# Values of a gated attention as a second seven-product unit, with operands resting in DRAM

## The chip, the cores and the metric

The kernel runs on one core of a Trainium2 chip (trn2). The metric is the device time of one execution in microseconds. The core's engines work from queues of their own and wait for each other by semaphores: TensorE (PE in the profile) multiplies, VectorE (DVE) and ScalarE (ACT) work elementwise and empty PSUM, GpSimd (POOL) does some elementwise work and issues transfers, SyncE (SP) issues transfers. Sixteen DMA engines move the data, for whichever queue.

## The reference

One decoder layer on 512 tokens of width 1024, in float32. What matters here is the token mixer's input projection, `h @ w_in`, and who reads its sections:

```python
q_g, k_g, v_g, r_g, a_lr, q_lat, kv_lat, gate_logits = jnp.split(h @ w_in, offsets, axis=-1)
o_gla = gla_chunked(q heads, k heads, v_g heads, log_a heads)      # gated linear attention, 4 heads
o_gla = rms_norm(o_gla, gla_norm_g)
y_gla = (o_gla * jax.nn.silu(r_g)) @ w_o_gla
q  = rms_norm(q_lat, q_a_norm_g) @ w_q_b                           # latents of the second attention
kv = rms_norm(kv_lat[..., :256], kv_a_norm_g) @ w_kv_b
```

`v_g` (the values) and `r_g` (the output gates before their silu) are both 512 x 1024 products of the normalised input, 512 x 1024, with 1024 x 1024 columns of `w_in`. After the mixer come an output projection, a layer norm, an MLP of width 4096 and a last layer norm.

## The kernel before

All large products are made from float32 operands that are split in a high and a low part (`split`, line 104, and line 180/181 for weights: ACT rounds the high part, DVE subtracts). A product is then three matmuls: high x high, high x low, low x high. Tokens stand in 4 tiles of 128 (`NT`), the width in 8 blocks of 128 (`NK`). `hT` holds the normalised input, transposed, as eight tiles with both parts.

*Weights* come as a stream planned ahead (`plan`, `pump`, lines 138 to 184): an entry is a pair of row blocks by up to 512 columns, 512 KB, loaded by SP into one of three `wraw` buffers, and split into `whi`/`wlo` or, where the entry's home is "a", into `xh`/`xl`.

*The seven-product unit.* The output gates `r` are made by `proj_r` (line 678) with a scheme of seven products in place of eight quarter products (Winograd's form of Strassen's). The input's rows (tokens) are taken as two halves of 256, its width as two halves of 512, the weight's columns as two halves of 512. `r_sums` (line 624) makes four sums and differences of the input's quarters, S1 to S4, each split in two tiles. The sums of weight quarters, T1 to T4, are made by transfers: `r_load` (line 612) loads a quarter on POOL's queue into a tile `rw`, and with `accum_op` adds another to what lies there. The order is `RPH`: T1, 11, 22, T2, 21, T3, T4; 11 and 21 are quarters of the weight itself and come through SP. T2 is made in T1's tile, T4 in T2's, T3 in 22's, each once the split of the tile before has been made. Seven products of 24 matmuls each accumulate in four PSUM banks; `put` (ACT) copies a bank out, `last` (DVE) adds a second one. `silus` (line 692) then turns the four result tiles `rg` into gates in place (ACT's tanh, line 697, DVE, line 698).

*The values* are made by `proj_v` (line 599): two plain GEMMs `gemm_tm` (line 246) of 512 columns over 8 row blocks and 4 token tiles. Each evacuation splits a PSUM bank straight into `vh` and `vl` (`split`, line 605).

*Side lanes.* Other work is written as generators that a `tick` (line 208) advances by one step, at most three of them at a time in this part (`WID`, line 1104): the levels of the gated attention (`gla_levels`, line 780, four heads one after the other), its outputs (`gla_out`, line 878, which wait for a head's levels, values and gates), and the silu. The GEMMs tick after each row block, `proj_r` eight times in all. A scheduler orders each engine's queue by priority, which is the order of the program, and by readiness in a model of the time; then each queue is fixed and runs in order. The sequence of sections is `ORDER` (line 288):

```python
ORDER = (("r", 0), ("v", 0), ("v", 1), ("g", 0), ("g", 2), ("qr", 0), ("g", 1), ("g", 3), ("qr", 1))
```

Here `g` are GEMMs of the branch gates and `qr` uses the latents. `latents2` (line 559) makes those: three tiles `qlT` and two `ckT` in `rms_T` (line 497).

*Memory.* All the tiles above except `hT`, `wraw`, `whi` and `wlo` share 24 slots of 4 KB per partition under the tag "A" (line 74): `s1` to `s4`, `rw`, `xh`/`xl`, `rg`, `vh`/`vl`, `latT`, `qk`, `kq`, `sd`, `KK`, the branch gates `gt`, `ogT`. A tile takes a slot when one is free and gives it back after its last reader.

Of the kernel before, what the change touches and what calls it, by code (L numbers as in the profile page):

```python
# [52 lines left out]
def tile_hybrid_block(ctx: ExitStack, tc: tile.TileContext, I, out, dbg=None):  # L53
# [24 lines left out]

    def S(shape, dt=F32, n="s"):
        return sm.tile(shape, dt, tag=n, name=nm(n))  # L80

    def MM(n="mm"):
        return pm.tile([P, T], F32, tag="mm", name=nm(n))
# [204 lines left out]
    ORDER = (("r", 0), ("v", 0), ("v", 1), ("g", 0), ("g", 2), ("qr", 0), ("g", 1), ("g", 3), ("qr", 1))  # L288

    RPH = ("T1", "11", "22", "T2", "21", "T3", "T4")  # L290
    RW = {}
    RAHEAD, RHOME = 2, "wawawawawawaww"

    def plan_qr(g):
        PL["qr", g] = plan("w_q_b", NOPE, 4 * ROPE, heads=(HQ, 4 * g, 4), per=4)

    for sec, i in ORDER:
        if sec == "v":
            PL["v", i] = plan("w_in", C_V + i * T, T)
        elif sec == "r":  # L300
            for n, op in enumerate(RPH):
                for hf in range(2):
                    PL["r", n, hf] = len(stream)
                    if op in ("11", "21"):
                        plan("w_in", C_R, T, 4 * (op == "21") + 2 * hf, 4 * (op == "21") + 2 * hf + 2)
                    else:
                        stream.append({"src": lambda q=(op, hf): RW[q], "nk": 2, "n": T, "res": False})
                    stream[-1].update(ahead=RAHEAD, home=RHOME[2 * n + hf])
# [287 lines left out]
    Rp = [None] * 2  # L596
    ogT = [None] * NK

    def proj_v(hp, guard=None):
        vp = []  # L600

        def e(a, j, ps):
            if a % 2 == 0:
                vp.append((A([P, 2, T], F32R, "vh"), A([P, 2, T], F32R, "vl")))
            split(ps, vp[-1][0][:, a % 2, :], vp[-1][1][:, a % 2, :])
            if a == NT - 1:
                Vp[hp] = vp
        gemm_tm([PL["v", hp]], hT, T, e, guard=guard)

    RS = {}  # L610

    def r_load(op, i, j, hf, add=False):
        w = I["w_in"].rearrange("(k p) n -> p k n", p=P)
        if not add:
            RW[op, hf] = A([P, 2, T], F32, "rw")
        k0 = 4 * i + 2 * hf
        nc.gpsimd.dma_start(RW[op, hf], w[:, k0:k0 + 2, C_R + j * T:C_R + (j + 1) * T], **({"accum_op": ALU.add} if add else {}))

    def r_add(dst, src, i, j):
        for hf in range(2):  # L620
            RW[dst, hf] = RW[src, hf]
            r_load(dst, i, j, hf, add=True)

    def r_sums():
        H, L = slice(0, 256), slice(256, T)
# [15 lines left out]
        RS["S1"] = pair("s1")  # L641
        for m in range(2):
            split(X[m], *[w[:, 2 * m:2 * m + 2] for w in RS["S1"]])
            yield
        RS["S4"] = pair("s4")
        for m in range(2):
            x = X[m]
            for kk in range(2):
                for w in range(2):
                    vtt(x[:, kk], x[:, kk], f(hT[2 * m + kk][:, w, H]), op=ALU.add)  # L650
            yield
            y = B([P, 2, 256], F32, "sy")
            for kk in range(2):
                k = 2 * m + kk
                vtt(y[:, kk], x[:, kk], f(hT[k + 4][:, 0, H]), op=ALU.subtract)
                vtt(y[:, kk], y[:, kk], f(hT[k + 4][:, 1, H]), op=ALU.subtract)
            yield
            split(y, *[w[:, 2 * m:2 * m + 2] for w in RS["S4"]])
            yield
        RS["S2"] = pair("s2")  # L660
        for m in range(2):
            c = slice(2 * m, 2 * m + 2)
            split(X[m], RS["S2"][0][:, c], RS["S2"][1][:, c], scale=-1.0)
            yield
        RS["S3"] = pair("s3")
        for m in range(2):
            c = slice(2 * m, 2 * m + 2)
            y = B([P, 2, 256], F32, "sy")
            for kk in range(2):
                k = 2 * m + kk  # L670
                t = B([P, 2, 256], F32, "st")
                vtt(t, f(hT[k][:, :, H]), f(hT[k][:, :, L]), op=ALU.subtract)
                vtt(y[:, kk], t[:, 0], t[:, 1], op=ALU.add)
            yield
            split(y, RS["S3"][0][:, c], RS["S3"][1][:, c])
            yield

    def proj_r():
        a, b = [MM() for _ in range(2)], None
        b = [MM() for _ in range(2)]  # L680
        R = {}

        def put(key, t, o, scale=1.0):
            if key not in R:
                R[key] = A([P, 2, T], F32, "rg")
            act(R[key][:, t], o, AF.Copy, scale=scale)

        def last(key, t, o, op):
            r = R[key][:, t]
            vtt(r, r, o, op=op)  # L690

        def silus():
            for key in ("12", "11", "22", "21"):
                for t in range(2):
                    r = R[key][:, t]
                    th = B([P, T], F32, "th")
                    act(th, r, AF.Tanh, scale=0.5)
                    stt(r, th, 1.0, r, op0=ALU.add, op1=ALU.mult)
                    yield
            Rp[0], Rp[1] = [R["11"], R["21"]], [R["12"], R["22"]]  # L700

        def lhs(n, k, t):
# [8 lines left out]
            while key not in RS:  # L711
                step(t_rs)
            return [w[:, k, c] for w in RS[key]]

        for n in range(7):
            o = a if n in (1, 3, 5) else b
            for hf in range(2):
                pump(PL["r", n, hf])
                for pp in range(2):
                    for t in range(2):  # L720
                        xh, xl = lhs(n, 2 * hf + pp, t)
                        hi, lo = [w[:, pp] for w in stream[PL["r", n, hf]]["w"]]
                        opens = n in (0, 1, 4, 6) and hf == 0 and pp == 0
                        mm(o[t], xh, hi, start=opens, stop=False, skip_group_check=True)
                        mm(o[t], xh, lo, start=False, stop=False, skip_group_check=True)
                        mm(o[t], xl, hi, start=False, stop=hf == 1 and pp == 1, skip_group_check=True)
                if hf == 0 and n in (0, 6):
                    tick(None)
                if n == 0 and hf == 1:
                    r_add("T2", "T1", 1, 1)  # L730
                if n == 2 and hf == 1:
                    r_add("T3", "22", 0, 1)
                if n == 3 and hf == 1:
                    r_add("T4", "T2", 1, 0)
            for t in range(2):
                if n == 0:
                    put("22", t, o[t], -1.0)
# [12 lines left out]
                    last("21", t, o[t], ALU.add)  # L750
            if n < 6:
                tick(None)
        return spawn(silus())

    SS = [None] * GH

# [121 lines left out]
    def gla_out(h):  # L878
        while SS[h] is None or Vp[h // 2] is None or Rp[h // 2] is None:
            yield  # L880
        sd, s128, kq = SS[h]

        def V(j):
            c = slice(h % 2 * HV, (h % 2 + 1) * HV)
# [34 lines left out]
        og = [B([P, 2, HV], F32, "og") for _ in range(2)]  # L919
        for i in range(NT):  # L920
            o = ps[i // 2][:, (i % 2) * HV:(i % 2 + 1) * HV]
            stt(og[i // 2][:, i % 2, :], o, rs[:, i:i + 1], Rp[h // 2][i // 2][:, i % 2, h % 2 * HV:(h % 2 + 1) * HV],
                op0=ALU.mult, op1=ALU.mult)
        yield
        for kk in range(2):
# [148 lines left out]
    for hf in range(2):  # L1074
        r_load("T1", 0, 1, hf)
    r_add("T1", "T1", 0, 0)
    RS["q"] = True
    gemm_fm(PL["q"], hT, T, ev_q, width=3)
    for hf in range(2):
        r_load("22", 1, 1, hf)  # L1080
    t_lat2 = spawn(latents2())
    gemm_fm(PL["k"], hT, T, ev_k, width=3)
    finish(t_prep, t_lat)
# [24 lines left out]
    def gates(br, mb):  # L1108
# [4 lines left out]
            act(gt[m][:, br, :], ps, AF.Tanh, scale=0.5, bias=hbg[:, br * NK + m:br * NK + m + 1])  # L1113
        gemm_fm(PL["g", br, mb], hT, T, ev_g)

    for sec, i in ORDER:
        if sec == "v":
            proj_v(i)
        elif sec == "r":
            proj_r()  # L1120
            finish(t_lat2)
        elif sec == "g":
            gates(i // 2, i % 2)
        else:
            mla_qr(i)
# [377 lines left out]
```

## Time and profile before

| | |
|---|---|
| median of 3 runs | 876.64 us (876.24 to 876.95) |
| the profiled execution | 876.98 us |
| its span, first to last instruction | 875.2 us |
| mean granted clock of TensorE | 0.998 |
| gates' unit on PE | 95.1 to 139.2 us |
| values on PE | 139.5 to 192 us |

A page of the profile tells one execution. A row of a group gives line, engine, operation, tiles out<-in, shape, count, then busy time and mean length of one in ns, then the engine's idle time before them and what ended it. A row by source line gives the lengths as min/median/max and the first and last start. A row of a stretch gives, for each engine, its busy time and the number of instructions, then the granted clock (PEclk), the share of time in which the 16 DMA engines were busy, and GB/s. A row of the timeline begins with start and length in us. PEld is the load of the stationary operand, which overlaps PE.

### The profile page before, as it was taken

How to read it: one execution, taken by the hardware profiler on the slowest of the kernel's cores; microseconds unless marked ns; L12 is line 12 of the kernel's file. 1: busy time of each engine (PE TensorE's matmuls, PEld its weight loads, DVE VectorE, ACT ScalarE, POOL GpSimd, SP SyncE). 2: the span in 40 equal slices, each digit the busy share in tenths (PEclk: the TensorE clock that was granted, in tenths of full speed). 3: DMA queues.
4: the chain of work that ended last, by engine and by line, in shares of the span. 5: the costliest groups of instructions: out<-in, count | busy, mean ns of one | idle time of the engine just before them, and what ended most of it. 6: DMA issues, size and time to landing. Idle time of an engine off the chain costs nothing. (4 is left out here: it accounts for less than half of the span.)

```text
span 875.2 us, 11522 instructions
## 1 busy us (share of the span) xinstructions
PE 857.4 (98%) x4312; PEld 730.7 (83%) x4312; DVE 595.6 (68%) x979; ACT 456.2 (52%) x788; POOL 163.9 (19%) x196
## 2 busy tenths in 40 slices
PE   5999999999999999999999999999999999999996
PEld 5988888888898888888888889988888888888885
DVE  6977998665564345557776888886567556753697
ACT  5367865454554343345555414566357546744662
POOL 2404753103011010000000012004400520242023
PEclk9999999999999999999999999999999999999999
DMA  6823572222222223121216537007931990398075
GB/s 225 244 59 124 109 154 73 72 83 70 84 73 73 67 66 121 31 67 57 95 64 248 169 102 260 1 1 193 282 103 37 260 254 28 67 314 196 0 186 104
DMA packets 65080, 105.34 MB, mean 120 GB/s; under 512 B 7905, under 2 KB 31892, under 8 KB 65024
## 3 DMA queue, kind: packets, MB, share of 16 engines
q1 hardware_dynamic: 47312, 61.94, 22.1%
q0 software_dynamic: 15792, 39.00, 19.2%
q10 hardware_dynamic: 1920, 3.66, 1.2%
q8 instruction: 34, 0.56, 0.3%
q14 instruction: 22, 0.18, 0.1%
HBM read 86.76 MB, written 3.67 MB: 103 GB/s over the span
## 5 line engine op out<-in xcount | busy, mean ns | idle before, releaser
L181 DVE TENSOR_TENSOR wlo<-wraw,whi 128x1024 fp32r<-128x1024 f32 (+2 forms) x96 | 109.3, 1139 | 128.4 <-ACT whi L180 122.4
L231 PE MATMUL mm<-h,whi 128*128 128x512 f32 x416 | 163.0, 393 | 0.0
L232 PE MATMUL mm<-h,whi 128*128 128x512 f32 x416 | 162.3, 390 | 0.0
L233 PE MATMUL mm<-h,wlo 128*128 128x512 f32 x416 | 155.0, 391 | 0.0
L180 ACT ACTIVATE whi<-wraw 128x1024 fp32r<-128x1024 f32 (+2 forms) x96 | 93.6, 975 | 100.3 <-PE mm L232 47.0
L1365 POOL DMA_DIRECT2D res<-ev x54 | 47.2, 983 | 238.5 <-ACT ev L1363 197.2
L233 PEld LDWEIGHTS mm<-h,wlo 128*128 128x128 f32 x416 | 78.0, 188 | 16.0
L231 PEld LDWEIGHTS mm<-h,whi 128*128 128x128 f32 x416 | 78.2, 188 | 15.6
L232 PEld LDWEIGHTS mm<-h,whi 128*128 128x128 f32 x416 | 78.2, 188 | 15.5
L1430 ACT ACTIVATE relu<-mm 128x512 f32<-128x512 f32 x32 | 18.8, 595 | 57.0 <-PE mm L233 57.0
L370 POOL TENSOR_TENSOR mv<-mv,mhalf 128x1 f32<-128x1 f32 x4 | 2.9, 744 | 208.1 <-DVE mv L369 208.1
L180 ACT ACTIVATE xh<-wraw 128x1024 fp32r<-128x1024 f32 (+1 forms) x22 | 21.1, 968 | 27.0 <-PE mm L266 15.8
L181 DVE TENSOR_TENSOR wlo<-wq,whi 128x1024 fp32r<-128x1024 f32 x15 | 18.4, 1224 | 20.4 <-ACT whi L180 20.4
L181 DVE TENSOR_TENSOR xl<-wraw,xh 128x1024 fp32r<-128x1024 f32 (+1 forms) x22 | 25.5, 1173 | 5.4 <-ACT xh L180 5.0
L810 ACT ACTIVATE M<-qk 128x256 f32<-128x256 f32 x56 | 23.9, 457 | 8.3 <-DVE qk L792 8.2
L792 DVE TENSOR_TENSOR qk<-qk,tot 128x512 f32<-128x512 f32 x28 | 21.5, 768 | 8.8 <-ACT M L810 6.3
L1280 POOL DMA_DIRECT2D wq<-in_w_ff_dram x32 | 24.0, 810 | 11.8 <-issue 5.9
L1363 ACT ACTIVATE ev<-mm 128x512 f32<-128x512 f32 x20 | 11.9, 600 | 27.5 <-DMA res<-ev 24.7
L231 PE MATMUL mm<-ogT,whi 128*128 128x512 f32 x64 | 25.7, 401 | 0.0
L232 PE MATMUL mm<-ogT,whi 128*128 128x512 f32 x64 | 25.3, 395 | 0.0
L232 PE MATMUL mm<-omT,whi 128*128 128x512 f32 x64 | 25.2, 394 | 0.0
L266 PE MATMUL mm<-whi,h 128*128 128x512 f32 x64 | 25.2, 393 | 0.0
(449 smaller groups left out, 2365.3 us busy)
## 6 DMA issues: line engine op xcount, KB each, us to landing
wraw<-in_w_in_dram SPq DMA_DIRECT2D x36, 512.0 KB, 3.6
wraw<-in_w_ff_dram SPq DMA_DIRECT2D x32, 512.0 KB, 8.2
wq<-in_w_ff_dram POOLq DMA_DIRECT2D x32, 512.0 KB, 9.2
res<-ev POOLq DMA_DIRECT2D x54, 256.0 KB, 9.0
rw<-in_w_in_dram POOLq DMA_DIRECT2D x12, 512.0 KB, 5.9
wraw<-in_w_o_gla_dram SPq DMA_DIRECT2D x8, 512.0 KB, 3.6
wraw<-in_w_o_mla_dram SPq DMA_DIRECT2D x8, 512.0 KB, 3.3
wraw<-in_w_out_dram SPq DMA_DIRECT2D x8, 512.0 KB, 4.0
```

The costliest lines, as they stand in the source:

```text
L180: st["ins"] = act(hi[:, :nk, :n], raw[:, :nk, :n], AF.Copy)
L181: vtt(lo[:, :nk, :n], raw[:, :nk, :n], f(hi[:, :nk, :n]), op=ALU.subtract)
L231: mm(o, hi[:, c], xh, start=first, stop=False)
L232: mm(o, hi[:, c], xl, start=False, stop=False)
L233: mm(o, lo[:, c], xh, start=False, stop=last)
L266: mm(o, xl, hi[:, :n], start=False, stop=last, skip_group_check=share)
L792: vtt(new, new, view(tot, o + 1, -1, 2, 0, s), op=ALU.mult)
L810: act(packed(M, s, i), half_lr(qk, s, i), AF.Copy)
L1280: nc.gpsimd.dma_start(t, w2[:, k0:k0 + 3:2, j * T:(j + 1) * T])
L1363: st["ev"] = act(e, o, AF.Copy, scale=-1.0 if ph == 4 else 1.0)
L1365: nc.gpsimd.dma_start(res[tt + t][:, j * T:(j + 1) * T], e, accum_op=ALU.add)
L1430: act(r, ps, AF.Relu)
```

## The change

The values become a second unit of the same kind, which reads the same S1 to S4. `proj_r` becomes `unit(sec, nxt)`, called once for "r" and once for "v"; `r_load`, `r_add` and the plan of the stream take the section as an argument. `ORDER` has one "v" in place of two.

What is kept for the second unit, or is not needed for a while, rests in DRAM tiles:

- each pair S1 to S4 is stored on SP's queue as soon as it is made (`keep`, eight transfers of 512 KB) and loaded again on POOL's queue (`fetch`, eight): S1 and S4 in the gates' sixth product, S2 and S3 in the values' first and third;
- the gates are stored after their silu (four transfers of 512 KB, SP), and each head's part is loaded when its output begins (two of 256 KB per head, SP);
- the five latent tiles are stored when they are made (SP) and loaded before the first `qr` (`fetch_lat`, POOL).

The first sum tiles of the values (T1: two loads and two adding loads, 22: two loads, all on POOL's queue) are issued from the gates' sixth and seventh products. In the value unit each result, once its second part has been added, is split from SBUF into `vh` and `vl`. The gates' unit ticks twice more (10 in all), the value unit 13 times, where the two value GEMMs ticked 16 times. The values of all heads are there at the end of the unit, where before the first two heads' were there after the first GEMM. The core of the diff:

```diff
+    dr = ctx.enter_context(tc.tile_pool(name="dr", bufs=1, space=bass.MemoryType.DRAM))
...
-    RAHEAD, RHOME = 2, "wawawawawawaww"
+    RAHEAD, RHOME = 2, {"r": "wawawawawawaww", "v": "wawawawawawaww"}
...
             split(p, o[:, 0, :], o[:, 1, :], scale=g[:, k:k + 1])
-            outs.append(o)
+            d = DR([P, 2, T], F32R, "latd")
+            nc.sync.dma_start(f(d), f(o))
+            outs.append(d)
...
-    def proj_v(hp, guard=None):
-        vp = []
-
-        def e(a, j, ps):
-            if a % 2 == 0:
-                vp.append((A([P, 2, T], F32R, "vh"), A([P, 2, T], F32R, "vl")))
-            split(ps, vp[-1][0][:, a % 2, :], vp[-1][1][:, a % 2, :])
-            if a == NT - 1:
-                Vp[hp] = vp
-        gemm_tm([PL["v", hp]], hT, T, e, guard=guard)
...
+    def r_begin(sec):
         for hf in range(2):
-            RW[dst, hf] = RW[src, hf]
-            r_load(dst, i, j, hf, add=True)
+            r_load(sec, "T1", 0, 1, hf)
+        r_add(sec, "T1", "T1", 0, 0)
+
+    def r_add(sec, dst, src, i, j):
+        for hf in range(2):
+            RW[sec, dst, hf] = RW[sec, src, hf]
+            r_load(sec, dst, i, j, hf, add=True)
+
+    KEPT = {}
+
+    def keep(name):
+        KEPT[name] = [DR([P, 4, 256], F32R, name) for _ in range(2)]
+        for d, w in zip(KEPT[name], RS[name]):
+            nc.sync.dma_start(f(d), f(w))
+
+    def fetch(name):
+        RS[name] = [A([P, 4, 256], F32R, name) for _ in range(2)]
+        for d, w in zip(KEPT[name], RS[name]):
+            nc.gpsimd.dma_start(w, d)
...
         def last(key, t, o, op):
             r = R[key][:, t]
             vtt(r, r, o, op=op)
+            if val:
+                if t == 0:
+                    R["v" + key] = [A([P, 2, T], F32R, n) for n in ("vh", "vl")]
+                split(r, *[w[:, t] for w in R["v" + key]])
...
+                d = DR([P, 2, T], F32, "rd")
+                nc.sync.dma_start(d, R[key])
+                R[key] = d
+                yield
...
-                if hf == 0 and n in (0, 6):
+                if hf == 0 and (val or n in (0, 2, 4, 6)):
                     tick(None)
                 if n == 0 and hf == 1:
-                    r_add("T2", "T1", 1, 1)
+                    r_add(sec, "T2", "T1", 1, 1)
+                    if val:
+                        fetch("S2")
                 if n == 2 and hf == 1:
-                    r_add("T3", "22", 0, 1)
+                    r_add(sec, "T3", "22", 0, 1)
+                    if val:
+                        fetch("S3")
                 if n == 3 and hf == 1:
-                    r_add("T4", "T2", 1, 0)
+                    r_add(sec, "T4", "T2", 1, 0)
+                if n == 5 and hf == 0 and nxt:
+                    r_begin(nxt)
+                    fetch("S1")
+                    fetch("S4")
+                if n == 6 and hf == 0 and nxt:
+                    for h2 in range(2):
+                        r_load(nxt, "22", 1, 1, h2)
...
+        rg = A([P, NT, HV], F32, "rg")
+        for i in range(2):
+            nc.sync.dma_start(rg[:, 2 * i:2 * i + 2], Rp[h // 2][i][:, :, h % 2 * HV:(h % 2 + 1) * HV])
...
+    def fetch_lat():
+        for l in (qlT, ckT):
+            for k in range(len(l)):
+                d, l[k] = l[k], A([P, 2, T], F32R, "latT")
+                nc.gpsimd.dma_start(l[k], d)
```

More of the change, by code (lines that the diff above doesn't have):

```diff
@@ L80, in S, with DR @@
         return sm.tile(shape, dt, tag=n, name=nm(n))
+    def DR(shape, dt=F32, n="dr"):
+        n = nm(n)
+        return dr.tile(shape, dt, tag=n, name=n)
     def MM(n="mm"):
@@ L643, in r_sums @@
             split(X[m], *[w[:, 2 * m:2 * m + 2] for w in RS["S1"]])
+            if m:
+                keep("S1")
             yield
@@ L658, in r_sums @@
             split(y, *[w[:, 2 * m:2 * m + 2] for w in RS["S4"]])
+            if m:
+                keep("S4")
             yield
@@ L675, in r_sums, with unit @@
             split(y, RS["S3"][0][:, c], RS["S3"][1][:, c])
+            if m:
+                keep("S3")
             yield
-    def proj_r():
-        a, b = [MM() for _ in range(2)], None
-        b = [MM() for _ in range(2)]
+    def unit(sec, nxt=None):
+        a, b = [[MM() for _ in range(2)] for _ in range(2)]
         R = {}
+        val = sec == "v"
         def put(key, t, o, scale=1.0):
@@ L710, in lhs @@
             key = {0: "S1", 2: "S4", 3: "S2", 5: "S3"}[n]
-            while key not in RS:
+            while not val and key not in RS:
                 step(t_rs)
@@ L721, in proj_r @@
                         xh, xl = lhs(n, 2 * hf + pp, t)
-                        hi, lo = [w[:, pp] for w in stream[PL["r", n, hf]]["w"]]
+                        hi, lo = [w[:, pp] for w in stream[PL[sec, n, hf]]["w"]]
                         opens = n in (0, 1, 4, 6) and hf == 0 and pp == 0
@@ L752, in proj_r @@
                 tick(None)
-        return spawn(silus())
+        if val:
+            for j in range(2):
+                Vp[j] = [R["v%d%d" % (i, j + 1)] for i in (1, 2)]
+        else:
+            t_sil.append(spawn(silus()))
     SS = [None] * GH
@@ L1073, in tile_hybrid_block @@
     t_lat = spawn(latents())
-    for hf in range(2):
-        r_load("T1", 0, 1, hf)
-    r_add("T1", "T1", 0, 0)
+    r_begin("r")
     RS["q"] = True
@@ L1079, in tile_hybrid_block @@
     for hf in range(2):
[L1080 removed]
+        r_load("r", "22", 1, 1, hf)
     t_lat2 = spawn(latents2())
@@ L1114, in gates @@
         gemm_fm(PL["g", br, mb], hT, T, ev_g)
-    for sec, i in ORDER:
[L1117 to L1121, printed above, removed]
+    def fetch_lat():
[3 more added lines that the diff above has]
+                nc.gpsimd.dma_start(l[k], d)
+    for sec, i in ORDER:
+        if sec == "qr" and i == 0:
+            fetch_lat()
+        if sec in "rv":
+            unit(sec, "v" if sec == "r" else None)
+            if sec == "r":
+                finish(t_lat2)
         elif sec == "g":
```

33 lines of the change are left out of this document (18 added, 15 removed).

## The prediction

> **What bounds the kernel now.** I read the page's busy lines first, then who TensorE (PE) waited for, then the busy time by stretch.
>
> ```profile
> span 875.2 us, 11522 instructions
> PE 857.4 (98%) x4312; PEld 730.7 (83%) x4312; DVE 595.6 (68%) x979; ACT 456.2 (52%) x788; POOL 163.9 (19%) x196
> DMA  6823572222222223121216537007931990398075
> ```
> ```profile
> PE px L385 <- ACT x L374: 8.3, 1, 8.3
> PE px L385 <- DVE x L376: 0.6, 1, 0.6
> PE mm L266 <- POOL h L393: 0.4, 1, 0.4
> ```
> ```profile
> core 0: us, PE busy (x) PEld busy (x) DVE busy (x) ACT busy (x) POOL busy (x), PEclk, DMA share, GB/s
> 600.00:700.00 100.00, 100.00 (x443) 82.84 (x442) 60.62 (x68) 54.94 (x77) 32.43 (x40) 1.00 0.67 182
> 95.00:139.20 44.20, 44.07 (x216) 36.81 (x216) 40.33 (x62) 28.10 (x47) 21.78 (x26) 1.00 0.51 108
> 139.20:191.90 52.70, 52.70 (x272) 44.67 (x271) 35.83 (x56) 28.29 (x60) 10.89 (x12) 1.00 0.30 90
> 250.00:284.00 34.00, 34.00 (x203) 29.82 (x203) 20.72 (x43) 16.44 (x35) 6.43 (x8) 1.00 0.26 78
> ```
> The reader should see that PE is busy 98% of the span, that its longest wait (8.3 us) lies at the start, and that no row names a wait in the stretches that the change touches, at a granted clock of 1.00. So PE's own work sets the end: a matmul that is left out shortens the time by its pitch, as long as nothing new makes PE wait. A hundred microseconds of nothing but 512-column matmuls hold 443, so the pitch is 100/443 = 0.226 us. (The 0.39 us that one matmul is shown with is not its price: they overlap.)
>
> ```profile
> L724 PE MATMUL mm<-whi,s x16: 389/389/478, 95.1 to 129.5; 128*128 128x512 f32 x16
> L266 PE MATMUL mm<-whi,h x64: 389/389/478, 140.3 to 192.1; 128*128 128x512 f32 x64
> ```
> The output gates' seven-product unit runs from 95.1 to 139.2, the two value GEMMs from there to 192. The first stretch is the model for what the values will look like: same products, same splits, VectorE (DVE) at 40.33 of 44.2 us (91%), and still no PE wait.
>
> **The change part by part.**
>
> *Matmuls.* Values now: 2 halves x 8 row blocks x 4 token tiles x 3 = 192 (L266's row: x64 for one of the three). Then: 7 products x 4 row blocks x 2 token tiles x 3 = 168. That is 24 fewer: 24 x 0.226 = **5.4 us** off PE. Nothing else is added to PE.
>
> [...]
>
> *VectorE in the value unit.*
> ```profile
> L181 DVE TENSOR_TENSOR wlo<-wraw,whi 128x1024 fp32r<-128x1024 f32 x8 | 10.9, 1359 | 6.6 <-ACT whi L180 6.6
> L698 DVE SCALAR_TENSOR_TENSOR rg<-th,rg 128x512 f32<-128x512 f32 x7 | 4.6, 688 | 0.0
> L107 DVE TENSOR_TENSOR vl<-mm,vh 128x512 fp32r<-128x512 f32 x6 | 4.0, 686 | 0.9 <-ACT vh L106 0.9
> L922 DVE SCALAR_TENSOR_TENSOR og<-px,grs,rg 128x256 f32<-128x256 f32 x4 | 1.7, 477 | 0.0
> L690 DVE TENSOR_TENSOR rg<-rg,mm 128x512 f32<-128x512 f32 x2 | 1.4, 689 | 0.0
> ```
> ```profile
> 117.85 2.51 DVE L792 TENSOR_TENSOR qk<-qk,tot 128x512 f32<-128x512 f32 x1 [1.68 <-ACT M L810]
> 120.28 0.42 DVE L817 COPY_PREDICATED SD<-cmask,px 128x256 f32<-128x256 uint8 x1
> 120.61 1.21 DVE L181 TENSOR_TENSOR wlo<-rw,whi 128x1024 fp32r<-128x1024 f32 x1
> 121.75 0.78 DVE L792 TENSOR_TENSOR qk<-qk,tot 128x512 f32<-128x512 f32 x1
> 122.45 2.31 DVE L181 TENSOR_TENSOR xl<-wraw,xh 128x1024 fp32r<-128x1024 f32 x1
> ```
> Neighbours overlap: a weight split of 1.21 us is followed after 1.14, and I price a 512-column operation at its 0.68 less the same 0.07, about 0.6. The unit needs 14 weight splits instead of 8 (14 x 1.14 = 16.0), 8 second halves added to the first (8 x 0.6 = 4.8), 8 value splits as before (4.8), and the gates' silu, 7 x 0.6 = 4.2. What is left of the 35.83 us of the second window is the levels of the gated attention: 35.83 less the splits 10.2, silu 4.2, values 3.6, outputs of head 0 1.6, last gate additions 1.2 and about 0.5 of small ones is 14.5 us in 16 ticks (steps of the side lanes). The unit gives 13 ticks: 11.8 us. Sum 41.6 us. The unit lasts 168 x 0.226 = 38.0 plus the PE work of the lanes, for which I take the first window's 44.2 - 38.0 = 6.2: **44.2 us**. So DVE stands at 94%, against 91% in the unit that never waits: I charge nothing, and at worst the overhang below. ScalarE (ACT) gets 6 more splits of weights and 8 more evacuations; its 28.1 of 44.2 leaves room.
>
> The row at 117.85 shows 2.51 us for an operation that took 0.78 at 121.75; GpSimd (POOL) was computing then (rows further down). [...] In the trace's own numbers: the stretches at 117.85 and 122.45 add 1.73 and 1.10 us; the same 2.8 again in the value unit makes 44.4 of 44.2 us, an overhang of 0.2.
>
> *Transfers.*
> ```profile
> q0 software_dynamic: 1371, 2.62, 35.7%
> q1 hardware_dynamic: 1088, 2.10, 14.5%
> ```
> ```profile
> q1 hardware_dynamic: 1360, 2.62, 25.8%
> ```
> ```profile
> out_dram<-bc SPq DMA_DIRECT2D x3, 512.0 KB, 3.6
> ```
> Two views of the queues: 95 to 139.2, then 250 to 284. In the first, POOL's queue moved five 512 KB transfers that add into a tile: 35.7% of 44.2 us / 5 = 3.15 us of all 16 DMA engines each. In the second, five plain loads: 25.8% of 34 / 5 = 1.75 us. Now the units' stretch (95 to 192) uses 0.51 x 44.2 + 0.30 x 52.7 = 38.3 us of DMA time. The change takes 8 value loads out (-14.0) and puts in 4 direct and 4 sum loads (+14.0), 8 adding ones (+25.2), 8 fetches of row sums (+14.0), 4 stores of gates (+7.0), the gate fetch of head 0 (+1.75) and the late stores (S3 and two latents, +7.0): 93.3 us in 96.9 - 5.4 = 91.5. A store into DRAM lands like a load (3.6 us). So the transfers would fill the stretch. The excess, 93.3 - 91.5 = **1.8 us**, is the one stall that I charge; bounds: 0 (gate stores and the next GEMM's loads can slip out of the stretch) and 6.7 (rivals).
>
> *Rest.* The other stores lie before 95, where the DMA line shows 2 to 7 tenths. The five latent fetches fall between 192 and 251 at a share near 0.26; cover: PE's gate GEMMs. If slots were late there, at most one landing on POOL's queue, 8.7 us (row below), would show; nearest row: no PE wait in that stretch, so 0. On SP a store waits for DVE's half of a split, and the weight loads queued behind wait with it: 0 to 3.6 us (a landing), taken as 0, because two splits of lead are kept. The heads' outputs start after the whole unit, not after half of the values:
> ```profile
> L110 DVE SCALAR_TENSOR_TENSOR ogT<-px,cb,ogT x8: 741/744/751, 195.4 to 298.1; 128x512 fp32r<-128x512 f32 x8
> L231 PE MATMUL mm<-ogT,whi x64: 387/389/481, 312.9 to 378.0; 128*128 128x512 f32 x64
> ```
> The last head's result is ready at 298.9 and used at 312.9. The last head follows the levels, whose ticks fall from 24 to 23 by the end of both units: one step later (12 matmuls, 2.7 us, and the lanes' own, some 3 us), with PE 5.4 earlier. 14.0 - 8.4 = 5.6 us of cover remain: no charge.
>
> *Sum.* -5.4 + 1.8 = -3.6. The profiled execution took 876.98 us, span 875.2 and 1.8 around it; the median is 876.64, 0.34 less. 876.6 - 3.6 = **873.0 us**.
>
> **The rivals.**
>
> *The first sum tile of the values comes late (slower).*
> ```profile
> L617 POOL DMA_DIRECT2D rw<-in_w_in_dram x6: 1194/1208/1247, 90.1 to 116.7; - x6
> DMA to landing us min/median/max: 5.5/6.3/8.7
> ```
> ```profile
> L181 DVE TENSOR_TENSOR wlo<-rw,whi x6: 1210/1216/1417, 90.5 to 132.5; 128x1024 fp32r<-128x1024 f32 x6
> ```
> ```profile
> 116.71 1.19 POOL L617 DMA_DIRECT2D rw<-in_w_in_dram  x1 [3.69 <-ACT xh L180]
> 117.47 1.09 POOL L767 TENSOR_TENSOR tot<-g 128x256 f32<-128x256 f32 x1
> ...
> 122.23 1.44 POOL L778 TENSOR_TENSOR qkp<-pr,qkp 128x512 fp32r<-128x512 f32 x1 [0.26 <-ACT qkp L777]
> 123.63 2.40 POOL L767 TENSOR_TENSOR tot<-tot 128x32 f32<-128x32 f32 x4
> ```
> Place: the seam of the units. The values' T1 is loaded, added to, and split before their first product: 1.2 + 6.3 + 1.2 + 6.3 for the two transfers and 2.3 for the split (ACT's half as the pitch of DVE's) = 17.3 us. To be in time for the seam at 139.5 the first load must leave POOL by 122.2: that is the point from which it decides. If its slot (line 74 has 24) is only free when the gates' last sum tile has been read, at 132.5 + 1.2 = 133.7, PE stands for 133.7 + 17.3 - 139.5 = 11.5 us: 871.2 + 11.5 = **882.7**. For it: sums, row sums and gates all ask for slots there. Against: by my count of the tiles alive at 115 some 20 of 24 are taken once the latents have left theirs, and POOL idled 3.7 us before 116.71. In between: a load that misses that gap finds POOL computing until 126 and costs 126 + 17.3 - 139.5 = 3.8 us: 875.0.
>
> *Transfers become the bound.* The adding transfers hang on splits, so the DMA engines will have holes. With 5% of holes the 93.3 us take 98.2, 6.7 more than 91.5: **877.9**. For it: 25 us of adding transfers. Against: the DMA line shows slices of 9 tenths later in the program without a PE wait.
>
> That the change doesn't do what it says is excluded by the products, which are counted in the code.
>
> **How the numbers follow.** Forecast 0.57 (own range 871.2, no stall, to 874.8); late T1 by POOL's order 0.06 (875.0); transfers as the bound 0.15 (877.9); late T1 by slots 0.22 (882.7; 878.5 to 883). A measurement of this kernel tells about 0.2% (1.75 us) from no change: faster means below 874.9, slower above 878.4. Faster 0.57, same 0.06 + 0.15 = 0.21, slower 0.22. The range runs from 870.8 (the bare saving less run-to-run spread) to 880.5: below it some 0.03, above it about 0.15 of the late-slot case.
>
> **What would show it.** Right: 24 fewer PE matmuls of 512 columns, gates and values together in about 91 to 94 us, PE waits in them under 2 us in all, DMA share near 1 there. The seam rival: a PE or weight-split wait at the values' first product, released by an adding transfer. The transfer rival: several waits of ACT on landings within the unit. Wrong altogether: PE waits outside 95 to 190, above all at 250 (latents) or 310 (outputs of the heads).

## The result and the profile after

| | us | against before |
|---|---|---|
| before, six runs beside it | 876.79 (876.24 to 877.48) | |
| changed kernel, six runs | 883.91 (883.45 to 884.41) | ratio 1.0081 [1.0068, 1.0094] |
| profiled execution, before / changed | span 875.2 / 881.7 | 6.5 longer |

The change makes the kernel slower by 7.1 us; forecast were 3.6 less. In the changed kernel the lines have moved: the splits of the weights (L180, L181) are L185 and L186, the load of the sum tiles (L617) is L614, the three products (L724 to L726) are L755 to L757, the fetch of the row sums is L636. Of the page: span, engines, clock and transfers.

```profile
span 881.7 us, 11628 instructions
PE 854.5 (97%) x4288; PEld 726.2 (82%) x4288; DVE 610.0 (69%) x993; ACT 466.2 (53%) x802; POOL 188.0 (21%) x221
PEclk9999998999999999999999999999999999999998
DMA  7836898933454223111307527006941990398075
```

The 24 matmuls are gone (4288 instead of 4312). The fifth to eighth slices of the DMA line (88 to 176 us), 5722 before, read 8989. Of the clock's slices within TensorE's work one, the seventh, is an 8 (the last one is an 8 too, where TensorE has ended). Now whom TensorE waited for in 95 to 200, and the two units by stretch:

```profile
PE mm L755 <- ACT whi L185: 5.1, 1, 5.1
PE mm L756 <- DVE wlo L186: 2.2, 2, 1.9
PE mm L755 <- ACT s L111: 0.6, 1, 0.6
```
```profile
core 0: us, PE busy (x) PEld busy (x) DVE busy (x) ACT busy (x) POOL busy (x), PEclk, DMA share, GB/s
95.00:140.20 45.20, 45.20 (x228) 38.14 (x228) 39.73 (x64) 28.94 (x51) 28.84 (x36) 1.00 0.94 246
140.20:145.50 5.30, 0.20 (x3) 0.01 (x1) 0.97 (x1) 2.06 (x3) 0.00 (x0) 0.80 0.89 320
145.50:150.20 4.70, 4.47 (x10) 3.08 (x11) 4.70 (x7) 3.87 (x8) 4.36 (x5) 0.50 0.20 17
150.20:189.00 38.80, 36.73 (x174) 30.00 (x173) 32.50 (x42) 23.14 (x40) 14.89 (x16) 1.00 0.87 229
```

The reader should see three things. At the seam of the units TensorE stands 5.1 us, for ScalarE's split of the values' first sum tile T1. When it goes on, it does so at a granted clock of 0.50, for 4.7 us, of which half, 2.4 us, is lost: ten matmuls in 4.7 us where the pitch of 0.226 would give 20. (The expectations below count 2.9 us for it.) And there is a second wait, 1.9 us near 172, for VectorE. Before, no wait of TensorE stood in 95 to 200.

The account by the profiled executions: waits 5.1 + 2.2 + 0.6 = 7.9, the slow clock 2.4, and 0.9 more behind the last matmul (below), less the 5.4 for the matmuls: +5.8 of the 6.5 us. Of the 0.7 left, 0.4 lies in the waits at the start of the program (10.0 us in sum, 9.6 before); the rest is not traced to a row.

Where T1's split was late, GpSimd's queue shows, in order of time:

```profile
117.88 1.21 POOL L614 DMA_DIRECT2D rw<-in_w_in_dram  x1 [1.78 <-DVE xl L186]
118.65 2.94 POOL L813 TENSOR_TENSOR tot<-tot 128x64 f32<-128x64 f32 x4
121.55 2.31 POOL L824 TENSOR_TENSOR qkp<-pr,qkp 128x512 fp32r<-128x512 f32 x1
123.82 1.18 POOL L813 TENSOR_TENSOR tot<-tot 128x4 f32<-128x4 f32 x1
124.94 1.50 POOL L614 DMA_DIRECT2D rw<-in_w_in_dram  x2
126.44 2.18 POOL L636 DMA_DIRECT2D S<-S  x4
129.77 4.07 POOL L614 DMA_DIRECT2D rw<-in_w_in_dram  x4 [1.15 <-DMA rw<-in_w_in_dram]
```
```profile
L614 POOL DMA_DIRECT2D rw<-in_w_in_dram x6: 742/1220/1233, 124.9 to 132.6; - x6
DMA to landing us min/median/max: 4.3/11.0/13.4
```

T1's two loads stand behind the totals and products of a level of the gated attention (118.65 to 124.9) and leave at 124.94, not by 122.2. Then four fetches of row sums go out ahead of T1's two adding loads (129.77 and 131.11), with two loads of another tile right behind. The second view is that of these six loads: the median landing is 11.0 us; T1's two adds took 9.7 and 12.3 us, and landed at 139.45 and 143.41. The load before them, at 117.88, took 6.5. The DMA engines were full: share 1.10 in 130 to 139, 1.07 in 139 to 144.

A second queue then makes it worse. ScalarE and VectorE around the seam:

```profile
143.44 1.06 ACT L185 ACTIVATE xh<-rw 128x1024 fp32r<-128x1024 f32 x1 [6.98 <-DMA rw<-in_w_in_dram]
144.40 1.04 ACT L185 ACTIVATE whi<-rw 128x1024 fp32r<-128x1024 f32 x1
```
```profile
136.87 0.68 DVE L838 TENSOR_TENSOR qk<-qk,g 128x512 f32<-128x512 f32 x1
144.53 1.23 DVE L186 TENSOR_TENSOR xl<-rw,xh 128x1024 fp32r<-128x1024 f32 x1 [6.98 <-ACT xh L185]
```

`whi` is the first half of T1, `xh` the second. ScalarE's queue has the second half first. So ScalarE stands 6.98 us for the landing at 143.41, with the first half, landed 4 us earlier, behind it, and VectorE stands as long behind ScalarE. The engine that the sum had watched as nearly full was idle 7 us because of its place in a line.

The wait at 172 is the same thing once more, one sum tile later. T2 is added into T1's tile, so it starts late too, and the later of its adds landed at 162.4. VectorE:

```profile
163.58 1.23 DVE L186 TENSOR_TENSOR wlo<-rw,whi 128x1024 fp32r<-128x1024 f32 x1 [5.92 <-ACT whi L185]
171.47 2.77 DVE L186 TENSOR_TENSOR wlo<-wraw,whi 128x1024 fp32r<-128x1024 f32 x1
```

VectorE stands 5.9 us for T2 and then works without a real pause; the split that TensorE waits for, of the next weight quarter, is the last in that line and takes 2.77 us where its neighbours take 1.2 to 1.3. GpSimd was busy for 9.7 us of 165 to 175.

### The profile page after: what moved, and what is told of

Same layout as the page of the kernel before. It is cut to its first block, busy times and chain, and to the rows that moved or that the text cites. A ratio compares the mean times of both kernels' runs of the same rounds, so it can differ in the third digit from the quotient of the medians.

```text
span 881.7 us, 11628 instructions
## 1 busy us (share of the span) xinstructions
PE 854.5 (97%) x4288; PEld 726.2 (82%) x4288; DVE 610.0 (69%) x993; ACT 466.2 (53%) x802; POOL 188.0 (21%) x221
## 5 line engine op out<-in xcount | busy, mean ns | idle before, releaser
L186 DVE TENSOR_TENSOR wlo<-wraw,whi 128x1024 fp32r<-128x1024 f32 (+2 forms) x90 | 102.2, 1137 | 97.8 <-ACT whi L185 92.0
L185 ACT ACTIVATE whi<-wraw 128x1024 fp32r<-128x1024 f32 (+2 forms) x90 | 87.0, 967 | 69.9 <-PE mm L237 34.5
L185 ACT ACTIVATE xh<-wraw 128x1024 fp32r<-128x1024 f32 (+1 forms) x24 | 23.2, 974 | 26.8 <-PE mm L271 15.4
L614 POOL DMA_DIRECT2D rw<-in_w_in_dram x24 | 26.1, 1128 | 32.6 <-DVE xl L186 12.9
L186 DVE TENSOR_TENSOR wlo<-wq,whi 128x1024 fp32r<-128x1024 f32 x15 | 18.4, 1224 | 19.9 <-ACT whi L185 19.9
L186 DVE TENSOR_TENSOR xl<-wraw,xh 128x1024 fp32r<-128x1024 f32 (+1 forms) x24 | 27.0, 1137 | 6.3 <-ACT xh L185 6.3
L838 DVE TENSOR_TENSOR qk<-qk,tot 128x512 f32<-128x512 f32 x28 | 23.5, 840 | 7.1 <-PE px L894 4.2
```

What stands on the lines that cost most here:

```text
L185: st["ins"] = act(hi[:, :nk, :n], raw[:, :nk, :n], AF.Copy)
L186: vtt(lo[:, :nk, :n], raw[:, :nk, :n], f(hi[:, :nk, :n]), op=ALU.subtract)
L614: nc.gpsimd.dma_start(RW[sec, op, hf], w[:, k0:k0 + 2, c0:c0 + T], **({"accum_op": ALU.add} if add else {}))
L838: vtt(new, new, view(tot, o + 1, -1, 2, 0, s), op=ALU.mult)
```

## The experiments

The theory that these lines suggest (A): no engine has too much to do, but T1 is late through the order of three queues (GpSimd's, the DMA engines', ScalarE's), and the clock adds to it. The rival (B): the unit is bound by full DMA engines or VectorE, and the seam is only the first place where that shows. The times of before beside these runs had medians of 877.0 to 877.3.

**T1 begun earlier.** One call moved:

```diff
+                if n == 2 and hf == 0 and nxt:
+                    r_begin(nxt)
                 if n == 5 and hf == 0 and nxt:
-                    r_begin(nxt)
                     fetch("S1")
                     fetch("S4")
```

> The values' first sum tile (T1) is begun in the third product of the gates instead of the sixth; nothing else moves by hand. Theory A (the stall of 5.3 us at the seam is T1's late landing, 139.45 and 143.41, because its loads left GpSimd's queue only at 124.9; the slow clock behind it, 2.9 us, comes with the idle): T1 is in SBUF before 135, the 5.3 and the 2.9 us go, the 2.2 us stall near 172 stays: 883.9 - 8.2 = 875.7 (875 to 877). Theory B (the values' unit is bound by VectorE and by full DMA engines, and the seam only shows it first): the wait comes back later within the unit, so at most half goes: 879 to 882. If T1's slots are not free so early, GpSimd's queue stands behind the load and the gates' own adding loads come late: slower than 884.

876.04 us, ratio to before 0.9985 [0.9976, 0.9995]: 7.9 us less than the changed kernel, as A said. GpSimd's queue and TensorE's waits:

```profile
112.38 2.69 POOL L614 DMA_DIRECT2D rw<-in_w_in_dram  x3 [0.82 <-DVE wlo L186]
...
124.44 1.21 POOL L614 DMA_DIRECT2D rw<-in_w_in_dram  x1 [3.91 <-DMA rw<-in_w_in_dram]
```
```profile
PE mm L756 <- DVE wlo L186: 1.9, 2, 1.4
PE mm L755 <- ACT s L111: 0.6, 1, 0.6
```

The first row holds the gates' own add and, without a pause, both loads of T1: their slots were free at 113, so the slots did not hold T1. The 5.1 us are gone, the clock stays at 1.00, and a wait of 1.4 us remains near 166.

**S4 fetched later.** T1 as in the changed kernel, two transfers fewer ahead of its adds:

```diff
                 if n == 5 and hf == 0 and nxt:
                     r_begin(nxt)
                     fetch("S1")
-                    fetch("S4")
...
+                if n == 0 and hf == 0 and val:
+                    fetch("S4")
```

> Order alone: the fetch of the row sums S4 (two transfers of 512 KB) is asked for in the first product of the values instead of ahead of T1's adding loads; T1 itself is begun as in the changed kernel. If the transfers ahead in a full set of DMA engines make the adds late: 2 x 1.75 = 3.5 us less ahead of them, the second add lands near 140 instead of 143.4, the seam costs about 2 us instead of 5.3 and the slow clock is shorter or gone: 878 to 881. If the order does not matter and only the late start of T1 does: within 1 us of 883.9. If S4 is then late itself: a new wait in the third product of the values, and nothing gained.

876.40 us, 0.9979 [0.9957, 1.0001]. More came back than the two transfers are worth:

```profile
PE px L892 <- ACT M L857: 1.4, 1, 1.4
PE mm L756 <- DVE wlo L186: 0.8, 1, 0.8
```

The adds landed at 137.9 and 140.5. The seam still costs about 2.4 us with its small gaps (TensorE's idle time in 139 to 150), but the slow clock and the wait near 172 are gone with the rest.

**Adding transfers that only write.** The kernel leaves out the sums of the values' weight quarters:

```diff
-        nc.gpsimd.dma_start(RW[sec, op, hf], w[:, k0:k0 + 2, c0:c0 + T], **({"accum_op": ALU.add} if add else {}))
+        nc.gpsimd.dma_start(RW[sec, op, hf], w[:, k0:k0 + 2, c0:c0 + T], **({"accum_op": ALU.add} if add and sec == "r" else {}))
```

> The values' adding transfers write instead of adding (same tiles, same bytes read, same queue and order), so the sums of the values' weight quarters are left out and the values are wrong. If the adding transfers' own time (3.15 against 1.75 us of all DMA engines) is what fills the engines: 8 x 1.4 = 11.2 us of demand less, landings back to about 4 to 6 us, the seam costs 1 to 3 us instead of 5.3, the stall at 172 goes: 876 to 880, with a DMA share under 1 in the unit. If the late start of T1 (124.9) and VectorE are what counts: the seam still costs 3 us or more, and the time is 881 to 884.

874.88 us, 0.9977 [0.9968, 0.9987]: 9.0 us less than the changed kernel, more than any single change of order, and under the 876 to 880 that was expected if the transfers' own time counts.

```profile
PE mm L755 <- ACT whi L185: 1.1, 1, 1.1
PE mm L756 <- DVE wlo L186: 0.7, 1, 0.7
```
```profile
144.00:147.40 3.40, 3.40 (x9) 2.65 (x9) 3.40 (x6) 2.19 (x5) 2.81 (x5) 0.50 0.47 87
```

The share of DMA time falls (0.93 in 150 to 170 instead of 1.08), T1 lands at 138.9 and 140.2. Even so the two waits of 1.1 and 0.7 us were answered by 3.4 us of half clock. So with the order as it was, the transfers' own time is a large part of the lateness, but shortening them alone does not cure the seam.

**ScalarE's order pinned.** One wait in the order of issue (the second half's split after the first's), no transfer touched:

```diff
-                    stream[-1].update(ahead=RAHEAD, home=RHOME[sec][2 * n + hf])
+                    stream[-1].update(ahead=RAHEAD, home=RHOME[sec][2 * n + hf], seq=sec == "v" and n == 0 and hf == 1)
...
-                for g in st["gates"]:
+                for g in st["gates"] + ((st["ins"],) if e.get("seq") else ()):
```

> The changed kernel with one order pinned on ScalarE: the first half of T1 (landed at 139.45) is split before the second (landed at 143.41); transfers, queues and their order stay. If half of the seam's stall is ScalarE and VectorE standing behind the wrong landing: first product near 140.6, waits of about 1 us for the low half and of 1 to 1.5 us for the second half, 2 to 3 us in all instead of 5.3, and the slow clock gone or 3.4 us long (1.5 us): 878.0 to 880.5. If the landings alone set the pace (the whole unit waits for the last add): within 1 us of 883.9.

876.47 us, 0.9984 [0.9970, 0.9998]: 7.4 us less, more than expected of it.

```profile
140.86 1.06 ACT L185 ACTIVATE whi<-rw 128x1024 fp32r<-128x1024 f32 x1 [2.97 <-DMA rw<-in_w_in_dram]
144.48 1.06 ACT L185 ACTIVATE xh<-rw 128x1024 fp32r<-128x1024 f32 x1 [2.56 <-DMA rw<-in_w_in_dram]
```

T1 landed no earlier here (140.8 and 144.5). What moved is what comes next. The first product, which begins on the first half alone, starts at 142.0 instead of 145.5. And T2 adds into T1's tile and can only go out when that half is split. Its first add left at 143.5 instead of 147.4, and the later of its two adds landed at 157.4 instead of 162.4.

**Useless matmuls in the gap.** 20 matmuls on a spare PSUM tile ahead of the values' first product:

```diff
...
+        if val:
+            wm = PX()
+            with tc.issue_after(st["rl"].ins):
+                for _ in range(20):
+                    nc.tensor.matmul(wm, hT[0][:, 0, :P], hT[0][:, 0, :], start=True, stop=True)
         for n in range(7):
...
```

> Twenty matmuls of no use (512 columns, 20 x 0.226 = 4.5 us) stand on TensorE between the last product of the gates and the first of the values, where it otherwise idles 5.3 us. If the granted clock of 0.50 for 6.8 us is the answer to that idle time: it stays at 1.00, and the kernel with 20 matmuls more takes about 2.9 us less, 881.0 (880.5 to 882). If the slow clock has another cause (the transfers, the load of all engines together), it comes all the same: 883.5 to 885.

885.10 us, 1.0091 [1.0076, 1.0106]. The expected saving did not come.

```profile
PE px L896 <- ACT M L861: 2.3, 2, 1.8
PE mm L760 <- ACT whi L185: 1.1, 1, 1.1
```
```profile
167.00:170.40 3.40, 3.40 (x12) 2.73 (x11) 3.40 (x5) 1.74 (x4) 3.40 (x5) 0.50 1.05 170
```

At the seam the clock does stay at 1.00. But T1 lands as late as ever, T2's later add lands at 162.4 as in the changed kernel, and TensorE, some 2 us of work further on by then, waits near 165 instead, this time with the half clock behind it. The idle time was not the cause but a slack of the chain of transfers: time won on TensorE alone was given back at the next landing.

**A pause in the kernel before.** To have the clock by itself, GpSimd copies ahead of the first value product of before, four or one, no transfer:

```diff
...
+                gp = B([P, T], F32, "gap")
+                nc.gpsimd.tensor_copy(gp, Rlast[0])
+                for _ in range(2):
+                    nc.gpsimd.tensor_copy(gp, gp)
+                gr = B([P, T], F32R, "gapr")
+                nc.gpsimd.tensor_copy(gr, gp)
+                gap.append(nc.tensor.matmul(PX(), gr[:, :P], hT[0][:, 0, :], start=True, stop=True))
...
```

The first value product is then issued after that last matmul, which reads GpSimd's copy.

> The kernel before, with one pause put in: after the last product of the gates TensorE waits for four GpSimd copies in a row (some 5 us) before the first value product; no transfer is added. If the slow clock after the changed kernel's seam is the answer to idle time alone: granted clock 0.50 for 3.4 or 6.8 us behind the pause, and the time rises by the pause plus 1.5 to 3.4 us. If the transfers cause the slow clock: clock 1.00 throughout, and the time rises by the pause only.

> The kernel before with a shorter pause: one GpSimd copy instead of four between the last product of the gates and the first value product, some 2 us. If the slow clock needs an idle stretch of more than about 3 us: clock 1.00, and the time rises by the pause alone, 878.5 to 879.5. If a shorter one is enough when it falls badly: 0.50 for 3.4 us in the profile and 880 to 881, or a wide spread between runs.

884.06 us, 1.0074 [1.0056, 1.0093], with four copies; 879.32, 1.0017 [1.0002, 1.0032], with one. The long pause and the clock behind it:

```profile
138.58 0.39 PE L102 MATMUL mm<-whi,h 128*128 128x512 f32 x1
143.66 0.79 PE L1134 MATMUL px<-h,gapr 128*128 128x512 f32 x1 [4.70 <-POOL gapr L1133]
```
```profile
143.60:148.80 5.20, 5.13 (x12) 4.07 (x13) 0.00 (x0) 0.00 (x0) 0.01 (x1) 0.50 0.16 60
```
```profile
PE px L1130 <- POOL gapr L1129: 1.5, 1, 1.5
```

4.7 us of idle time brought 0.50 for 6.8 us (142.0 to 148.8, in the trace), and the kernel lost 7 us, the pause and half of the 5.2 us behind it. The 1.5 us of the short pause (last row) left the clock at 1.00 in the profiled execution (878.33 us; the median is 1.0 longer, which no trace explains). So the slow clock needs none of the transfers that the change adds: here it followed 4.7 us of idle time. In the units and behind the long pause the slow stretches are 3.4 or 6.8 us long (table below), at 0.50.

**Both orders together.** T1 early and S4 late, the two diffs above in one kernel:

> Both orders together: T1 begun in the third product of the gates, the fetch of S4 asked for in the first product of the values. The two runs with one of them each left 3.4 and 3.1 us of TensorE loss more than before in 90 to 200. If these are two places of one queue (the seam in the one, a wait near 165 in the other), both go: loss within 1 us of before, 876.6 - 5.4 + 1 = 872.2 (871.5 to 874). If the transfers as a whole are the bound of the unit (share 1.08 to 1.10), moving them only moves the wait: 875.5 to 877, as with one of them.

872.45 us, 0.9943 [0.9924, 0.9962].

```profile
95.00:139.00 44.00, 43.64 (x217) 36.83 (x218) 42.34 (x66) 31.71 (x56) 26.89 (x36) 1.00 0.99 267
139.00:144.00 5.00, 5.00 (x28) 4.23 (x27) 5.00 (x8) 4.05 (x9) 4.37 (x5) 1.00 1.10 306
144.00:150.00 6.00, 6.00 (x30) 5.05 (x29) 6.00 (x10) 3.89 (x7) 1.33 (x2) 1.00 1.11 328
150.00:170.00 20.00, 20.00 (x97) 16.81 (x97) 18.76 (x24) 15.67 (x28) 10.62 (x14) 1.00 1.10 285
```
```profile
PE mm L755 <- ACT s L111: 0.6, 1, 0.6
```

This decides between A and B, as to what bounds the kernel. The same transfers, the same splits, the DMA engines at 1.10 through 139 to 170 and VectorE at 29.8 of 31 us (the last three windows), and TensorE waits for nothing in them. Full is not late. The kernel beats both others: 4.6 us under before, 11.5 under the changed one.

**Fewer transfers besides.** The same, with S1 and S3 left in SBUF, eight transfers less:

```diff
-            if m:
-                keep("S1")
...
-            if m:
-                keep("S3")
...
-                    fetch("S1")
...
-                    if val:
-                        fetch("S3")
```

> As the run with both orders, and the row sums S1 and S3 stay in SBUF from the gates to the values (no store, no fetch: 8 transfers of 512 KB less, 8 x 1.75 = 14 us of all DMA engines). If the transfers still bound the unit: 1 to 2 us faster than with the two orders alone, 871 to 873, DMA share under 1. If order was all: the same as that run. If four tiles more for so long leave no slot for T1: the seam stall is back, 878 or more.

872.42 us, 0.9942 [0.9923, 0.9960]: no difference from the run above. With the order right, 4 MB fewer are worth nothing, though the share stays between 0.87 and 1.09 in 130 to 170.

**The resting alone.** The values by the two GEMMs of before; gates, latents and row sums still go to DRAM:

```diff
-    ORDER = (("r", 0), ("v", 0), ("g", 0), ("g", 2), ("qr", 0), ("g", 1), ("g", 3), ("qr", 1))
+    ORDER = (("r", 0), ("v", 0), ("v", 1), ("g", 0), ("g", 2), ("qr", 0), ("g", 1), ("g", 3), ("qr", 1))
...
-        if sec in "rv":
-            unit(sec, "v" if sec == "r" else None)
+        if sec == "v":
+            proj_v(i)
+        elif sec == "r":
+            unit(sec)
```

> The changed kernel with the values by the two GEMMs of before (192 matmuls, no sum tiles, no fetch of row sums); finished output gates, latents and row sums still go to DRAM, and gates and latents come back. If the resting costs nothing by itself, as the sum had it: the time of before, 876.0 to 877.5, no PE wait over 1 us in 130 to 200. If the stores on SP's queue or the fetches collide: 878 to 881 with waits at SP's weight loads, at the latents (250) or at the heads' outputs (310).

878.29 us, 1.0002 [0.9978, 1.0026], and in 95 to 200 one PE wait, the 0.6 us at the gates' first product. The interval includes no change, but the median lies 1.2 us above that of before (877.10), all ten runs lie above 29 of the 31 of before, and the 876.0 to 877.5 expected was missed. The span's median is only 0.6 us longer (875.85 against 875.3); the other half stands outside the span of first to last instruction, and no trace shows its cause. So the resting costs about 1 us, and none of it as a wait of TensorE in the two units.

**Fetches on another queue.** On top of both orders, the fetches of the latents (first line), then of the row sums too (both), are issued from SP, to see what sets the end of the program:

```diff
-                nc.gpsimd.dma_start(l[k], d)
+                nc.sync.dma_start(f(l[k]), f(d))
...
-            nc.gpsimd.dma_start(w, d)
+            nc.sync.dma_start(f(w), f(d))
```

GpSimd's last instructions, of before and of the changed kernel:

```profile
L1499 POOLq DRAIN  x3: 51/93/4887, 869.3 to 874.9; - x3
```
```profile
L1553 POOLq DRAIN  x3: 51/102/6057, 874.8 to 881.4; - x3
```

The longest drain took 4.9 us in the one, 6.1 in the other, both begun 2 us behind the last matmul. In the changed kernel it is the last to end (880.9); in before SyncE's closing steps end 0.3 us after it (874.4). So 0.9 of the 1.2 us show at the end.

> The run with both orders, with the five fetches of the latents issued from SP's queue instead of GpSimd's (128 transfers on GpSimd's queue instead of 133). In the profiles so far GpSimd's closing drain takes 4.9 to 5.0 us with 108 to 113 transfers on its queue, 5.9 with 129, 6.0 to 6.2 with 133, some 45 ns each above 108, and the program ends with it. If it goes with their number: drain 5.7 to 5.8 us, and 0.2 to 0.3 us less than the 872.45 us. If SP's weight loads stand behind a fetch that waits for a slot: PE waits near 230 to 250, 873 to 876.

> As the one before, and the eight fetches of row sums on SP's queue too (120 transfers on GpSimd's queue). If the drain goes with their number: 5.3 to 5.5 us, about 0.6 us less than with both orders, 871.9, and T1's adding loads leave GpSimd's queue a little earlier. If a fetch that waits for its slot holds the weight loads behind it on SP: PE waits within 95 to 190 and 874 or more.

872.41 us, 0.9950 [0.9933, 0.9966], drain 5.8; and 873.36, 0.9957 [0.9942, 0.9972], drain 5.9. The first drain came about as expected, but the kernel gained nothing that can be told from 872.45. The second refutes the count: with 120 transfers on GpSimd's queue the drain should have been 5.3 to 5.5. What makes it longer stays open.

The changed kernel and the runs that touch its seam, by the chain there (times in the trace; the clock is the length of granted 0.50 in the units):

| run | T1's adds landed | first product | T2's first add left | half clock | us |
|---|---|---|---|---|---|
| changed kernel | 139.4, 143.4 | 145.5 | 147.4 | 6.8 | 883.91 |
| useless matmuls | 140.1, 143.7 | 145.8 | 147.7 | 3.4 | 885.10 |
| no adding | 138.9, 140.2 | 142.3 | 144.2 | 3.4 | 874.88 |
| ScalarE's order | 140.8, 144.5 | 142.0 | 143.5 | 0 | 876.47 |
| S4 late | 137.9, 140.5 | 143.1 | 143.2 | 0 | 876.40 |
| T1 early | 132.2, 134.7 | 140.9 | 140.6 | 0 | 876.04 |
| both orders | 132.4, 134.9 | 140.6 | 139.3 | 0 | 872.45 |

## Why the prediction was wrong

*The matmuls.* Right. 24 are gone, and with the order mended the last one starts at 861.5 instead of 867.0: 5.5 us earlier, against 5.4 in the sum.

*VectorE.* Right in size. 29.8 of 31 us in the run with both orders is 96%, without a wait; the sum had 94%. Where it was waited for (1.9 us at 172 in the changed kernel), it had itself stood 5.9 us for T2, up to 163.6.

*Transfers.* The demand was put too high, 93.3 us of DMA time in 91.5. The run with both orders used a share of 0.91 of it, 83 us (0.99 in 95 to 139, 1.10 in 139 to 170, 0.24 in 170 to 180):

```profile
95.00:186.50 91.50, 91.14 (x450) 76.87 (x451) 87.96 (x128) 65.68 (x116) 44.18 (x57) 1.00 0.91 248
```

So the 1.8 us charged had no ground, and nothing of it shows in that run. What came with the full DMA engines (1.10 and 1.07 in 130 to 144 of the changed kernel) is the later landing, 9.7 and 12.3 us for T1's adds where 6.3 was taken, and that entered no term of the forecast.

*The step that failed* is the seam: "the first sum tile of the values comes late" was a rival, deciding at 122.2, and the forecast took T1 to be in time. The load left at 124.94. That is the rival's middle case ("a load that misses that gap finds POOL computing until 126"), which had a chance of 0.06 and a price of 3.8 us. The chance of 0.22 stood on the slots, which the run with T1 early shows free at 113; that its 882.7 lies near the measured 883.91 is luck. The gap before 116.71, counted against the rival, was no offer: GpSimd's queue is in a fixed order, and the loads stood behind the totals in it. The list of instructions ahead of the load should have been the argument, not the idle time.

*The price.* The chain of 17.3 us has two errors that nearly cancel. It counts 1.2 us of issuing beside each landing, but the landing is counted from the start of the issue (131.11 + 12.3 = 143.4, and ScalarE, standing for it, starts at 143.44): 2.4 too much. And its landings of 6.3 come from a stretch whose share was 0.51; at 1.10 T1's adds took 9.7 and 12.3. So the first half landed 14.5 us after its load had left, where the chain has 15.0: luck. What made the price too small came behind that. ScalarE's order put the half that landed last in front, so the first product came at 145.5, where 124.94 + 17.3 gives 142.2. The sum had no clock: 2.4 us for the half speed behind the pause. And it had no second wait: the 1.9 us at 172 is T2's lateness, handed on through VectorE's queue.

*The transfer rival* (877.9) had the cause wrong: with the order right the DMA engines bind nothing, they only made a late chain later (by much: 9.0 us came back when the adds only wrote). *The rest* held for TensorE: no new wait at 250 or at the heads' outputs. *Not foreseen*: 0.9 us at the end of the program, 0.6 at the gates' first product in every variant of the changed kernel, and the 1.2 us by which the resting alone is slower (the 0.6 may be part of it).

## What to carry to other kernels

For a tile made by a chain of transfers, write down what stands ahead of each link (on the issuing engine, on the DMA engines, on the engine that consumes it), take the landing at the share that the stretch will have after the change (6.3 us at 0.51, but 9.7 and 12.3 at 1.10 and 1.09 here), and ask in which order two halves are consumed. Three single reorderings, one of them of two ScalarE instructions with no transfer touched, each took back 7.4 to 7.9 us, and both orders together 11.5. Cheaper transfers took back 9.0 with the order left as it was; removing transfers took back nothing once the order was right. And price the clock behind a TensorE pause: those of 5.1 and 4.7 us cost half as much again here, 2.4 and 2.6 us at 0.50. Filling the pause with useless work did not help (885.10 against 883.91), since the chain behind it had not moved.

## What the hardware showed beyond expectation

- Behind an idle TensorE the granted clock was 0.50 for 3.4 or 6.8 us in some runs and 1.00 in others: 5.1 us (changed kernel) and 4.7 us (the long pause) of idle time were each followed by 6.8 us of half clock, 1.5 us (the short pause) by none. Between these the length of a wait doesn't decide alone: 1.8 us brought 3.4 us of half clock in the run with useless matmuls and 1.9 us near 172 none in the changed kernel; 1.1 and 0.7, within 141.2 to 143.8, brought 3.4 in the run without adding and 1.4 and 0.8, within 140.8 to 144.7, none with S4 late.
- In the trace of the changed kernel the clock changes at 143.40, 150.23 and 877.27 us, so 6.83 and 727.0 us apart: 2 and 213 times 3.413. The 3.41 us ahead of the half clock held 1.83 us of idle time (163.6 to 167.0, useless matmuls) and 1.86 (140.6 to 144.0, no adding). The steps of 3.41 us counted on from 150.23 in the changed kernel have one with 1.77 (170.7 to 174.1), and the clock stays at 1.00 behind it. What makes the difference was not shown.
- 512 KB through GpSimd's queue landed in 6.3 us (median of six transfers for sum tiles of before, where the share was 0.51) and in 9.7, 12.3 and 13.1 at 1.07 to 1.10 (T1's adds and the later one of T2 in the changed kernel); single ones stayed shorter (7.2 for T2's first add in the kernel with both orders, at 1.10), and the kernel with both orders hides it all.
- GpSimd's closing drain grew from 4.9 to 6.1 us, and the changed kernel ends with it. It did not follow the number of transfers on that queue (5.9 us with 120, 5.8 with 128, 6.0 with 133, 5.0 with 113).
